# Fourier/Hyena encoder layer: where the first filter taps stand on ScalarE, how six weight halves get their low part, and when stored weight parts leave

## The chip, the cores and the metric

The kernel runs on one core of a Trainium2 chip. The metric is the device time of the program in microseconds (us): the median of three runs. The core's engines work side by side, each through its own list of instructions in a fixed order: TensorE (PE, matmuls), VectorE (DVE), ScalarE (ACT), GpSimd (POOL) and SyncE (SP, which only issues DMAs). DMAs are issued on the queue of SP or of POOL. An engine stops at an instruction whose input isn't there, and all that stands behind that instruction stops with it.

## What is computed

One encoder layer on two sequences of 1024 tokens by 1024 channels, in float32. The reference, cut to the steps that matter here:

```python
xn = rmsnorm(x, g_pre)
p = xn @ w_in
fv, fg, hv, hg, mg = jnp.split(p, [...], axis=-1)
fz = fv.reshape(B, L, F_GROUPS, F_GROUP_DIM)
fz = jnp.fft.fftn(fz, axes=(1, 3), norm="ortho").real        # Fourier branch
y_f = (fz.reshape(B, L, F_WIDTH) * jax.nn.silu(fg)) @ w_fourier_out
hv = short_conv(hv, w_short)                                 # Hyena branch
v, x1, x2 = jnp.split(hv, 3, axis=-1)
h = jnp.sin(f2 * (jnp.sin(f1 * (z @ w1 + b1)) @ w2 + b2))
h = (h @ w3) * jnp.exp(-t * jnp.abs(decay))                  # filter taps
h = h / jnp.sum(jnp.abs(h), axis=(0, 1))
kf = jnp.fft.rfft(two_sided(h))                              # filter spectrum
z = v
for n, gate in enumerate((x1, x2)):
    z = gate * long_conv(z, kf[:, n], hyena_d[n])
y_h = (z * jax.nn.silu(hg)) @ w_hyena_out
g_f, g_h = jnp.split(jax.nn.sigmoid(mg + b_merge), 2, axis=-1)
return x + rmsnorm((g_f * y_f + g_h * y_h) @ w_out, g_post)
```

All of it ends up as matrix products on PE, the Fourier transforms too.

## The kernel before

**Number format.** PE takes float32 rounded to fewer bits ("fp32r"). To keep float32 accuracy each operand is kept as two parts: a high part h, the rounded copy, and a low part l = source - h. A product takes three matmuls, h·h, l·h and h·l. `split` (lines 171 and 181) makes the parts: ACT copies (CAST) and another engine, DVE by default in this region, subtracts.

**Stages.** `phase_fourier` transforms both sequences. For the second, its last stretch goes from about 200 us to 258 us: a product `pfx` (PE, 16 matmuls) fills a small tile that ACT copies to `x5t` (line 411), DVE subtracts a part of it in place, and the closing matmuls of the products `pse` ("alt, x5t") read it. Each product `pse` is copied by ACT to `sev` (line 434), and DVE joins that with the odd half `pso`. The results leave as `d_fz` stores on POOL's queue (lines 486 and 487).

`phase_main` follows, and its opening is interleaved with that last stretch of the Fourier phase:

- `load_x` loads eight tiles of x into xl0_0 to xl0_7 (line 722, SP's queue); ACT casts each into xh0_k (1.04 us), DVE subtracts.
- `hid`, the filter's hidden layer, is loaded, cast by ACT (line 916), and a part of it is subtracted by DVE.
- `filter_taps` runs 16 rounds. A round casts its weights `w3s`, takes the absolute value of `dec` (line 632), does exponentials `ex` (line 643, behind a table load the first time), products `pft` on PE, and multiplications and sums on DVE, and `filter_spectrum` then makes products `pXf`.
- Between the rounds `spill_gate` computes in-projection gates, as filler: one gate in round 0, two in round 1, and so on. In the order in which PE reaches them I call the first five A, B, C, D and E.

**In-projection** (`inproj`, lines 743 to 769). A gate uses two weight half tiles of 128 x 1024 in two pieces, each 128 x 512 values wide. For each: SP loads it raw into `wr` (line 760, two slots, taken in turn), ACT casts it to the high part (line 764), ACT writes its negative into the low part (line 765, "mul"), and POOL issues a DMA that reads the weight from memory once more and adds it to that negative in place (line 766, an accumulating DMA). The high and low part stand in `wh` and `wl` (two slots each) or in one of two single slots for both, `whl`, according to `rooms`, whose turn goes wh, wh, whl (`draw`), whl (`draw2`), and round again. So gate A has wh and wh, gate B the two whl slots, C has wh and wh, D the two whl slots again. PE does 8 matmuls of x with each piece's high and 4 with its low part per 512 columns of tokens: 24 matmuls for a half tile, 48 for a gate.

`keep_parts` (lines 736 to 741): for sections whose parts are needed again for the second sequence, the parts are stored in memory (`d_w`, line 739, POOL's queue), and the stores are issued when the next half tile's accumulating DMA has been issued.

**What sets the order.** The kernel is written as loops; a scheduler with its own model of times then fixes the order of each engine's list. A block `with tc.issue_after(ins)` makes the instructions in it that run on the engine of `ins` stand behind `ins`. The order within SP's and POOL's DMA queues comes from that same step.

Of the kernel before, what the change touches and what calls it, by code (L numbers as in the profile page):

```python
# [9 lines left out]
F32 = mybir.dt.float32  # L10
# [151 lines left out]
class K:  # L162
# [223 lines left out]
    def fourier_half(self, b, half, W, fo, px, pf, begun={}):  # L386

        nc = self.nc
# [5 lines left out]
        for e, (W_, n, X_) in enumerate(((WE, 260, EE), (WO, 256, OO))):  # L394
            for m in range(4):
# [6 lines left out]
                if e == (b + half == 0):  # L402

                    if m == 0:
                        p5 = self.psum("X", 2, "pfx")[0:36, :260]
# [2 lines left out]
                            self.mm(p5, fo["x5"][:, k], WE[i][:, k], k + i == 0, k + i == 8)  # L408

        X5, XX, PX = fo["x5t"], fo["xx"], fo["px"]  # L410
        nc.scalar.copy(X5[0:36], p5)
        self.sub("dve", X5[32:36], p5[32:36], X5[32:36])

        EX = fo["ex"]
# [8 lines left out]
        def stage(np_, data, e, edge, out, tag):  # L423

            pe = self.psum(tag, 2, "pse")[0:np_, :258]
            po = self.psum(tag, 2, "pso")[0:np_, :258]
            for m in range(4):
                last = (edge is None and m == 1) or m == 3
                self.mm3(pe if m < 2 else po, data(m), (seq[:, 0, e, m], seq[:, 1, e, m]), m % 2 == 0, last)
                if m == 1 and edge is not None:  # L430
                    self.mm(pe.rearrange("p (a b) -> p a b", a=3), edge, al, False, True)
            ev = pf.tile([P, 258], F32, tag="sev", name="sev", bufs=1)[0:np_]
            st = pf.tile([P, 514], F32, tag="sst", name="sst", bufs=1)[0:np_]
            nc.scalar.copy(ev, pe)
            self.add("dve", st[:, 0:258], ev, po)
            if e == 0:
                self.sub("dve", st[:, 512:257:-1], ev[:, 0:255], po[:, 0:255])
            else:
                self.stt("dve", st[:, 512:257:-1], ev[:, 0:255], -1.0, po[:, 0:255])
            nc.vector.tensor_copy(st[:, 513:514], st[:, 0:1])  # L440
            if len(out) == 2:
                self.split(out[0], out[1], st, "dve", "act")
            else:
                nc.scalar.copy(out[0][0:34], st)
                self.sub("dve", out[0][32:34], st[32:34], out[0][32:34])
# [3 lines left out]
        for g in range(2):  # L449
            cs = slice(130 * g, 130 * g + P)  # L450
            PP.append(pair([P, 514], "pp", 2))
            stage(P, lambda m: (EE[0][:, m, cs], EE[1][:, m, cs]), 0, X5[:, cs], PP[g], "TX"[g])
        stage(34, lambda m: (EX[0][:, m], EX[1][:, m]), 0, XX, [PX], "T")
        for g in range(2):
            Pp, Qp = PP[g], pair([P, 514], "qp")
            co = slice(P * g, P * g + P)
            stage(P, lambda m: (OO[0][:, m, co], OO[1][:, m, co]), 1, None, Qp, "XT"[g])
            A = pf.tile([P, 1026], F32, tag="fAB", name="fA", bufs=3)
            B = pf.tile([P, 1026], F32, tag="fAB", name="fB", bufs=3)
            gg = 2 * half + g  # L460
            for n in range(2):
# [17 lines left out]
                r = slice(0, w)  # L479
# [3 lines left out]
                r = slice(0, w)  # L483
# [249 lines left out]
        t = pool.tile([P, 2, 512], F32R, tag=tag, name="whl", bufs=1)  # L733
        return [t[:, 0], t[:, 1]]

    def keep_parts(self):

        for t, k in self.unsaved:
            self.nc.gpsimd.dma_start(k, t.bitcast(F32))
        self.unsaved = []  # L740

    def inproj(self, sec, mt, b=None, plain=False):

        nc, a = self.nc, self.a
        ps = [self.psum("mm", 4, f"pin{n}") for n in range(2)]
        for q in range(2):
            s = slice(512 * q, 512 * q + 512)
            src = a["w_in"][sec, mt][:, s]
            kept = self.d_w[sec - 1][mt] if b is not None else None
            if b or plain:  # L750
                h, l = [self.wp.tile([P, 512], F32R, tag=g, name=g, bufs=2) for g in ("wh", "wl")]
            else:
                h, l = self.rooms()
            if b:
                self.keep_parts()
                for t, k in zip((h, l), kept):
                    nc.sync.dma_start(t.bitcast(F32), k[:, s])
            else:
                r = self.wp.tile([P, 512], F32, tag="w", name="wr", bufs=2)
                nc.sync.dma_start(r, src)  # L760
                if plain:
                    self.split(h, l, r, "dve", "act")
                else:
                    nc.scalar.copy(h, r)
                    nc.scalar.mul(l, h, -1.0)
                    self.added = nc.gpsimd.dma_start(l, src, accum_op=ADD)
                    self.keep_parts()
                    if kept:
                        self.unsaved = [(t, k[:, s]) for t, k in zip((h, l), kept)]
            h, l = [t.rearrange("p (a b) -> p a b", a=4) for t in (h, l)]  # L770
            for n in range(2):
                for kk in range(4):
                    k = 4 * q + kk
                    s = slice(512 * n, 512 * n + 512)
                    self.mm3(ps[n], (h[:, kk], l[:, kk]), (self.xh[k][:, s], self.xl[k][:, s]), k == 0, k == 7)
        return ps
# [127 lines left out]
    def phase_main(self, nct=8, nb=NB, nf=16):  # L904
        tc, nc, a = self.tc, self.nc, self.a
        with ExitStack() as es:
            pool = lambda n: es.enter_context(tc.tile_pool(name=n, bufs=1, reuse_waits="tile"))
            mf, wa, wb, mi = pool("mf"), pool("wa"), pool("wb"), pool("mi")
            self.stage2 = pool("m2")
            self.turn, self.unsaved = 3, []  # L910
            ws = Rooms(wa, wb)
            self.load_x(0, range(4))
            self.hid = ws.tile([P, L], F32R, tag="q", name="hid", bufs=2)
            hid = ws.tile([P, L], F32, tag="q", name="hidr", bufs=2)
            nc.sync.dma_start(hid, self.d_h)
            nc.scalar.copy(self.hid, hid)
            self.sub("dve", self.hid[64:128], hid[64:128], self.hid[64:128])
            taps = self.filter_taps(0, 0, ws)
            self.load_x(0, range(4, 8))
            self.cfw0 = mf.tile([P, 4 * P], F32, name="cfw0")  # L920
            self.cfwd = mf.tile([P, 2, 12 * P], F32R, name="cfwd")
            nc.sync.dma_start(self.cfw0, a["c_fw0"])
            nc.gpsimd.tensor_copy(self.cfwd[:, 0, 0:1], self.xl[4][:, 0:1])
            nc.gpsimd.dma_start(self.cfwd, a["c_fwd"])
            for t, n in ((self.th, "c_th"), (self.wsh, "w_short"), (self.bm, "b_merge")):
                nc.sync.dma_start(t, a[n])
            plain = [(5, c) for c in range(8)] + [(6, c) for c in range(8)] + [(4, c) for c in range(NH)]
            fill = sorted([((2 * c + 1) / len(plain), t) for c, t in enumerate(plain)]
                          + [((2 * c + 1) / max(NF, 1), (0, c)) for c in range(NF)])
            fill = [t for _, t in fill]  # L930
            for i in range(nf):
                nxt = self.filter_taps((i + 1) % 2, (i + 1) // 2, ws) if i + 1 < nf else None
                gates = fill[i * len(fill) // nf:(i + 1) * len(fill) // nf]
                if i < nf - 1:
                    self.filter_spectrum(i % 2, i // 2, taps, ws)
                for sec, c in gates:
                    self.spill_gate(0, sec, c, ws)
                if i == nf - 1:
                    first = [self.conv(1 + n, 0, ws, "vx"[n], 0, True) for n in range(2)]
                    self.filter_spectrum(i % 2, i // 2, taps, ws)  # L940
                taps = nxt
                if i == 4:
                    self.cinv = mi.tile([P, 2, INVW], F32R, name="cinv")
                if 4 <= i < 12:
                    w = slice((i - 4) * INVW // 8, (i - 3) * INVW // 8)
                    with tc.issue_after(self.added.ins):
                        nc.gpsimd.dma_start(self.cinv[:, :, w], a["c_inv"][:, :, w])
            self.branches(nb, nct, ws, *first)
# [576 lines left out]
```

## Time and profile before

| quantity | value |
|---|---|
| median of 3 runs | 2421.94 us |
| the runs | 2418.77 to 2423.49 us |
| the profiled execution's own time | 2420.15 us |
| its span in the trace | 2418.3 us |
| busy share of the span: PE, DVE, ACT, POOL | 98 %, 82 %, 47 %, 19 % |

The span is what the trace covers of one execution; 1.85 us lie around it. A row of a timeline has the start in us, the duration in us, the engine, the line of the program, the operation, its output and inputs, shapes, and how many instructions are joined; in brackets stands how long the engine had been idle just before, and what ended that. A row of a window table has the stretch, its length, then the busy us and the count of instructions for PE, PE's weight loads, DVE, ACT and POOL, then the clock that PE was granted (1.00 is full speed), the DMA share and GB/s. A row of the DMA view ends with the size and the median time from issue to landing.

### The profile page before, as it was taken

Reading aid. Unit: us, or ns where it says so; the run is one execution under the profiler, and the core shown is the slowest. Engines: PE = TensorE matmul, PEld = TensorE weight load, DVE = VectorE, ACT = ScalarE, POOL = GpSimd, SP = SyncE. Lnnn points to the kernel's source line nnn. Section 1 sums busy time; section 2 is a strip of 40 time slices with the busy share of each in tenths; the row PEclk is TensorE's granted clock in tenths of the full one; section 3 lists DMA queues with packets and bytes.
Section 4 is the critical chain, followed back from the end, with each engine's and each line's share of the span. In section 5 each row is a group of like instructions: output and inputs, shape, how many; then the busy total and the mean of one; then the engine's idle time right before and its main releaser. Section 6 shows DMA issues by size and latency. Waiting matters only on the chain. (4 is left out here: it accounts for less than half of the span.)

```text
span 2418.3 us, 37119 instructions
## 1 busy us (share of the span) xinstructions
PE 2360.6 (98%) x13006; PEld 2050.7 (85%) x13006; DVE 1976.0 (82%) x3760; ACT 1147.7 (47%) x2140; POOL 447.5 (19%) x575
## 2 busy tenths in 40 slices
PE   6999899999999999999999999999999999999998
PEld 6998788888888888888888888888878888888886
DVE  7786888888737999899899999997666687777787
ACT  6546666666544444344222322333344475656543
POOL 1331111111123332221023454310000000101000
PEclk9999899999999999999999999999999999999999
DMA  7536688787778777666365666553546687888754
GB/s 277 187 127 220 179 222 222 202 225 215 202 219 254 221 223 209 192 177 200 126 194 191 210 218 205 187 179 123 205 158 230 210 298 256 267 270 230 222 159 154
DMA packets 265010, 499.63 MB, mean 207 GB/s; under 512 B 26662, under 2 KB 92423, under 8 KB 264568
## 3 DMA queue, kind: packets, MB, share of 16 engines
q1 hardware_dynamic: 220076, 380.53, 48.0%
q0 software_dynamic: 44560, 116.72, 19.0%
q8 instruction: 102, 1.67, 0.3%
q14 instruction: 84, 0.69, 0.1%
q10 hardware_dynamic: 188, 0.02, 0.0%
HBM read 333.59 MB, written 167.77 MB: 207 GB/s over the span
## 5 line engine op out<-in xcount | busy, mean ns | idle before, releaser
L194 PE MATMUL pin<-xh,wh 128*128 128x512 f32 x1024 | 401.2, 393 | 0.4 <-DMA wh<-d_w 0.4
L194 PE MATMUL pin<-xl,wh 128*128 128x512 f32 x1024 | 401.2, 392 | 0.0
L194 PE MATMUL pin<-xh,wl 128*128 128x512 f32 x1024 | 399.6, 392 | 0.0
L194 PE MATMUL pin<-xh,whl 128*128 128x512 f32 x896 | 292.4, 397 | 8.1 <-DMA whl<-in_w_in 4.5
L194 PEld LDWEIGHTS pin<-xh,wh 128*128 128x128 f32 x1024 | 192.8, 188 | 35.9 <-DMA wh<-d_w 0.8
L194 PEld LDWEIGHTS pin<-xh,wl 128*128 128x128 f32 x1024 | 192.7, 188 | 35.6 <-DMA wl<-in_w_in 0.2
L194 PEld LDWEIGHTS pin<-xl,wh 128*128 128x128 f32 x1024 | 192.7, 188 | 34.8
L194 PEld LDWEIGHTS pin<-xh,whl 128*128 128x128 f32 x896 | 168.3, 190 | 42.8 <-DMA whl<-in_w_in 5.2
L194 PE MATMUL pT<-cinv,yh 128*128 128x256 f32 x1024 | 192.9, 283 | 2.7 <-ACT yh L171 2.7
L194 PE MATMUL pin<-xl,whl 128*128 128x512 f32 x448 | 178.1, 398 | 0.0
L194 PEld LDWEIGHTS pT<-cinv,yh 128*128 128x128 f32 x1024 | 165.4, 191 | 12.9 <-ACT yh L171 3.2
L194 PE MATMUL pX<-bh,cfwd 128*128 128x256 f32 x768 | 159.3, 287 | 0.9 <-ACT bh L171 0.9
L181 DVE TENSOR_TENSOR t<-pX,k 128x1024 f32<-128x1024 f32 x128 | 155.7, 1216 | 3.9 <-PE pX L194 2.9
L171 ACT CAST yh<-y 128x512 fp32r<-128x512 f32 x128 | 79.3, 620 | 152.8 <-DVE y L181 113.1
L194 PE MATMUL pT<-cinv,yl 128*128 128x256 f32 x512 | 145.5, 284 | 0.0
L171 ACT CAST bh<-b 128x512 fp32r<-128x512 f32 x144 | 88.9, 619 | 98.3 <-DVE b L181 58.1
L194 PEld LDWEIGHTS pX<-bh,cfwd 128*128 128x128 f32 x768 | 125.8, 191 | 4.6 <-ACT bh L171 1.3
L181 POOL TENSOR_TENSOR draw<-draw 128x256 f32<-128x256 f32 x96 | 93.8, 977 | 112.1 <-DMA draw<-in_w_out 39.5
L181 DVE TENSOR_TENSOR bl<-b,bh 128x512 fp32r<-128x512 f32 x144 | 100.3, 703 | 11.5 <-ACT bh L171 11.4
L194 PE MATMUL pX<-bl,cfwd 128*128 128x256 f32 x384 | 109.5, 285 | 0.0
L181 DVE TENSOR_TENSOR yl<-y,yh 128x512 fp32r<-128x512 f32 x128 | 90.2, 705 | 16.9 <-ACT yh L171 16.5
L194 PEld LDWEIGHTS pT<-cinv,yl 128*128 128x128 f32 x512 | 98.2, 192 | 1.9
(368 smaller groups left out, 6030.0 us busy)
## 6 DMA issues: line engine op xcount, KB each, us to landing
k<-d_k SPq DMA_DIRECT2D x128, 512.0 KB, 4.6
wr<-in_w_in SPq DMA_DIRECT2D x136, 256.0 KB, 3.6
d_g<-gt SPq DMA_DIRECT2D x92, 256.0 KB, 3.3
d_k<-kt SPq DMA_DIRECT2D x128, 128.0 KB, 3.7
d_k<-kt SPq DMA_DIRECT2D x64, 256.0 KB, 3.6
fz<-d_g SPq DMA_DIRECT2D x64, 256.0 KB, 5.1
wl<-in_w_in POOLq DMA_DIRECT2D x56, 256.0 KB, 5.4
whl<-in_w_in POOLq DMA_DIRECT2D x56, 256.0 KB, 5.7
```

The lines of the kernel that those rows point to most:

```text
L171: self.rounded = nc.scalar.copy(h, src)
L181: return e.tensor_tensor(out, a, b, op=op)
L194: return self.nc.tensor.matmul(out, lhsT, rhs, start=start, stop=stop, skip_group_check=shared)
```

## The change

Three parts. In the first, the cast of `hid` is put behind the copy `x5t` on ACT (`self.edge`), and ACT's part of the first round of `filter_taps` behind the second copy `sev` (`self.evens[1]`). In the second, for the gates of rounds 0 and 1 (A, B and C, six half tiles), `split` is used: the low part is a subtraction by GpSimd from the raw tile and its high part, in place of ACT's negative and the accumulating DMA. In the third, `keep_parts` leaves the newest half tile's stores unissued, so that in the code they come one half tile later than they did.

```diff
@@ -408,7 +408,8 @@
-        nc.scalar.copy(X5[0:36], p5)
+        self.edge = nc.scalar.copy(X5[0:36], p5)
+        self.evens = []
@@ -431,7 +432,7 @@
-            nc.scalar.copy(ev, pe)
+            self.evens.append(nc.scalar.copy(ev, pe))
@@ -733,11 +734,11 @@
-    def keep_parts(self):
+    def keep_parts(self, left=0):
 
-        for t, k in self.unsaved:
-            self.nc.gpsimd.dma_start(k, t.bitcast(F32))
-        self.unsaved = []
+        while len(self.unsaved) > left:
+            for t, k in self.unsaved.pop(0):
+                self.nc.gpsimd.dma_start(k, t.bitcast(F32))
@@ -758,15 +759,14 @@
-                if plain:
-                    self.split(h, l, r, "dve", "act")
+                if plain or self.opening:
+                    self.split(h, l, r, "dve" if plain else "pool", "act")
                 else:
                     nc.scalar.copy(h, r)
                     nc.scalar.mul(l, h, -1.0)
                     self.added = nc.gpsimd.dma_start(l, src, accum_op=ADD)
-                    self.keep_parts()
-                    if kept:
-                        self.unsaved = [(t, k[:, s]) for t, k in zip((h, l), kept)]
+                    self.keep_parts(1)
+                    self.unsaved.append([(t, k[:, s]) for t, k in zip((h, l), kept or ())])
@@ -913,9 +913,11 @@
-            nc.scalar.copy(self.hid, hid)
+            with tc.issue_after(self.edge.ins):
+                nc.scalar.copy(self.hid, hid)
             self.sub("dve", self.hid[64:128], hid[64:128], self.hid[64:128])
-            taps = self.filter_taps(0, 0, ws)
+            with tc.issue_after(self.evens[1].ins):
+                taps = self.filter_taps(0, 0, ws)
@@ -929,6 +931,7 @@
             for i in range(nf):
+                self.opening = i < 2
```

The lines of the changed kernel are one to three higher than those of before from here on.

Three places in the engines' lists show what moves. First, **ACT** where the Fourier copies and the first taps meet (about 204 to 217 us in the trace of before). Before, from the last cast of `oo` on:

```order
L171 CAST oo0_2487<-pfv1_2695 128x256
L916 CAST hid_2985<-hidr_2986 128x1024
L171 CAST w3s_2993<-w3_2990 128x256
L632 ACTIVATE dec_2996<-dec_2996 128x256
L411 CAST x5t_279<-pfx_2516 36x260
L643 ACT_TABLE_LOAD
L643 ACTIVATE ex_3003<-dec_2996,vec_68 128x256 x2
L643 ACTIVATE ex_3013<-dec_2996,vec_68 128x256 x2
L434 COPY sev_2747<-pse_2732 128x258
L171 CAST xh0_0_2965<-xl0_0_2966 128x1024
L434 COPY sev_2772<-pse_2757 128x258
L171 CAST xh0_1_2970<-xl0_1_2971 128x1024
```

And of the change, on the same engine from `x5t` on:

```order
L411 CAST x5t_279<-pfx_2516 36x260
L917 CAST hid_2985<-hidr_2986 128x1024
L435 COPY sev_2747<-pse_2732 128x258
L171 CAST xh0_0_2965<-xl0_0_2966 128x1024
L435 COPY sev_2772<-pse_2757 128x258
L171 CAST w3s_2993<-w3_2990 128x256
L171 CAST pp0_2730<-sst_2748 128x514
L633 ACTIVATE dec_2996<-dec_2996 128x256
L644 ACT_TABLE_LOAD
L644 ACTIVATE ex_3003<-dec_2996,vec_68 128x256 x2
L644 ACTIVATE ex_3013<-dec_2996,vec_68 128x256 x2
L171 CAST xh0_1_2970<-xl0_1_2971 128x1024
```

`x5t` now stands ahead of `hid` and the taps' start; the taps' start stands behind the second `sev`, which itself stands behind the cast of xh0_0; and xh0_1 now stands behind the table load and the exponentials, while xh0_0 keeps its place right behind the first `sev`.

Second, **POOL** (about 190 to 277 us): the accumulating DMAs of the first weight pieces, with the `d_fz` stores between them. Before:

```order
L766 DMA wl_3286<-in_w_in 128x512
L766 DMA wl_3317<-in_w_in 128x512
L766 DMA whl_3554<-in_w_in 128x512
L486 DMA d_fz1_4_105<-fA_2261 128x1024
L487 DMA d_fz1_5_106<-fB_2262 128x1024
...
L766 DMA wl_3631<-in_w_in 128x512
L766 DMA wl_3662<-in_w_in 128x512
L766 DMA whl_3899<-in_w_in 128x512
...
L766 DMA whl_3584<-in_w_in 128x512
L766 DMA wl_3968<-in_w_in 128x512
L766 DMA wl_3999<-in_w_in 128x512
L766 DMA whl_3929<-in_w_in 128x512
```

And of the change (whl_3552 and whl_3581 are B's two pieces, whl_3893 and whl_3923 are D's, wl_3962 and wl_3993 are E's):

```order
L181 TENSOR_TENSOR wl_3286<-wr_3287,wh_3285 128x512
L181 TENSOR_TENSOR wl_3316<-wr_3317,wh_3315 128x512
L181 TENSOR_TENSOR whl_3552<-wr_3553,whl_3552 128x512
L487 DMA d_fz1_4_105<-fA_2261 128x1024
...
L181 TENSOR_TENSOR wl_3627<-wr_3628,wh_3626 128x512
L181 TENSOR_TENSOR wl_3657<-wr_3658,wh_3656 128x512
...
L767 DMA whl_3893<-in_w_in 128x512
...
L181 TENSOR_TENSOR whl_3581<-wr_3582,whl_3581 128x512
L767 DMA wl_3962<-in_w_in 128x512
L767 DMA wl_3993<-in_w_in 128x512
L767 DMA whl_3923<-in_w_in 128x512
```

Six DMAs became six subtractions, in the same places but for D's first piece, which went behind two of the `d_fz` stores. From E's wl on, POOL's list is the same row for row as before, the numbers in the names apart; the stores of line 739 stand where they stood.

Third, **PE** behind gate B's second piece (about 274 to 282 us). Before:

```order
L194 MATMUL pin1_3553<-xh0_7_3071,whl_3584 128x512
L655 MATMUL pn_3143<-acc_3095,ones_73 128x128
L656 MATMUL pn_3143<-ones_73,acc_3095 128x2
L194 MATMUL pft_3365<-w3s_3356,hid_2985 128x256 x4
L194 MATMUL pXf_3195<-b0_3163,cfw0_3076 128x128 x4
L194 MATMUL pXf_3217<-bh_3173,cfwd_3077 128x256
L194 MATMUL pin0_3897<-xh0_0_2965,whl_3899 128x512
```

And of the change, whose first row is the last but one of D's first piece, which there follows on B's second piece directly:

```order
L194 MATMUL pin0_3891<-xl0_3_2981,whl_3893 128x512
L194 MATMUL pin0_3891<-xh0_3_2980,whl_3893 128x512
L194 MATMUL pin0_3891<-xh0_4_3056,whl_3923 128x512
L194 MATMUL pin0_3891<-xl0_4_3057,whl_3923 128x512
L194 MATMUL pXf_3195<-b0_3163,cfw0_3076 128x128 x4
L194 MATMUL pXf_3217<-bh_3173,cfwd_3077 128x256
L194 MATMUL pin0_3891<-xh0_4_3056,whl_3923 128x512
```

The sum `pn`, the products `pft_3365` (now `pft_3363`), the rest of `pXf_3217` and the eight `pft` of two further tiles stood ahead of the matmuls with the low part of D's second piece before, and stand behind them now.

## The prediction

> **What bounds the kernel now.** I read first the page's busy times, then a table of windows, then PE's timeline in the one window that isn't full, then the lists of the engines that PE waits for there.
>
> ```profile
> span 2418.3 us, 37119 instructions
> ...
> PE 2360.6 (98%) x13006; PEld 2050.7 (85%) x13006; DVE 1976.0 (82%) x3760; ACT 1147.7 (47%) x2140; POOL 447.5 (19%) x575
> ```
>
> ```profile
> 200.00:285.00 85.00, 70.52 (x376) 59.65 (x376) 61.67 (x130) 50.03 (x98) 10.05 (x15) 0.88 0.64 197
> 285.00:660.00 375.00, 375.00 (x2077) 326.27 (x2076) 312.48 (x760) 253.60 (x552) 46.84 (x57) 1.00 0.79 216
> ```
>
> PE bounds nearly everything: from 285 to 660 us it is busy for all of 375 us at full clock. The change touches the stretch from 200 to 285 us, where PE stands still for 85 - 70.52 = 14.5 us and has a mean clock of 0.88. By the clock at most 0.12 x 85 = 10 us more are lost, some of it during the idle time. About 20 us are the **ceiling** of what the change can win. Two groups of gaps make it up. The first:
>
> ```profile
> 206.14 0.96 PE L194 MATMUL pse<-seq,ee 128*128 128x258 f32 x6
> 209.56 0.51 PE L194 MATMUL pse<-alt,x5t 128*128 128x258 f32 x2 [2.46 <-DVE x5t L181]
> ...
> 212.38 1.50 PE L194 MATMUL pse<-seq,ex 128*34 128x258 f32 x6 [1.50 <-ACT sev L434]
> ...
> 215.18 1.05 PE L194 MATMUL pin<-xh,wh 128*128 128x512 f32 x2
> ...
> 219.69 0.63 PE L194 MATMUL pin<-xh,wh 128*128 128x512 f32 x2
> ```
>
> PE waits 2.46 us for x5t and 1.50 us for the first sev; at 215.18 gate A starts on tile 0 of x, at 219.69 on tile 1. The second group:
>
> ```profile
> 256.96 0.73 PE L194 MATMUL pft<-w3s,hid 128*128 128x256 f32 x4 [1.40 <-DVE T L181]
> 261.31 0.80 PE L194 MATMUL pin<-xh,whl 128*128 128x512 f32 x1 [3.62 <-ACT whl L764]
> ...
> 267.90 1.22 PE L194 MATMUL pin<-xh,whl 128*128 128x512 f32 x2 [4.51 <-DMA whl<-in_w_in]
> ...
> 274.49 0.38 PE L655 MATMUL pn<-acc,ones 128*128 128x128 f32 x2
> ...
> 275.41 1.05 PE L194 MATMUL pXf<-b,cfw 128*128 128x128 f32 x8
> ...
> 276.42 0.39 PE L194 MATMUL pin<-xh,whl 128*128 128x512 f32 x1
> ...
> 279.68 0.28 PE L194 MATMUL pXf<-bl,cfwd 128*128 128x256 f32 x1
> ...
> 281.96 0.63 PE L194 MATMUL pin<-xh,whl 128*128 128x512 f32 x2
> ```
>
> PE waits 3.62 us for the cast of gate B's second piece (whl) and 4.51 us for the accumulating DMA of its low part. The last row is the low part of gate D's second piece, which waits for nothing.
>
> **First part: the Fourier copies first.** ACT's list there:
>
> ```profile
> 205.75 1.05 ACT L916 CAST hid<-hidr 128x1024 fp32r<-128x1024 f32 x1 [1.72 <-DMA hidr<-d_h]
> 206.71 0.40 ACT L171 CAST w3s<-w 128x256 fp32r<-128x256 f32 x1
> 208.38 0.42 ACT L632 ACTIVATE dec<-dec 128x256 f32<-128x256 f32 x1 [1.27 <-DMA dec<-in_filt_decay]
> 208.70 0.35 ACT L411 CAST x5t<-pfx 36x260 fp32r<-36x260 f32 x1
> 209.07 1.28 ACT L643 ACT_TABLE_LOAD   x1
> 210.37 1.70 ACT L643 ACTIVATE ex<-dec,vec 128x256 f32<-128x256 f32 x4
> ...
> 212.23 1.04 ACT L171 CAST xh<-xl 128x1024 fp32r<-128x1024 f32 x1
> ```
>
> x5t's copy stood behind a wait for `dec`. Now it runs when its product is done, at about 206.2 instead of 208.7, and DVE's subtraction behind it is ready 0.86 us later (209.56 - 208.70), at 207.1, which is when PE is through with the product before it (206.14 + 0.96): the 2.46 us go. Then hid takes 1.05 us on ACT, sev follows at about 207.6, and the product at 212.38 starts near 208.3, **some 4 us earlier**. But what is late next is tile 0:
>
> ```profile
> 204.12 0.43 SPq L722 DMA_DIRECT2D xl<-d_x  x1
> ```
>
> ```profile
> xl<-d_x SPq DMA_DIRECT2D x1, 512.0 KB, 7.8
> ```
>
> It lands at 204.12 + 7.8 = 211.9, as before; its cast ends near 213.0, so gate A starts at 213.0 instead of 215.18. The product itself takes no longer than 215.18 - 212.38 = 2.8, so PE idles from 211.1 or before. Behind that cast, ACT now does sev, w3s (0.40), pp0, dec (0.42), the table load (1.28) and four exponentials (1.70) before it comes to tile 1: 213.0 + 4.3 + 1.05 = 218.4, while PE's work on tile 0, 4.5 us before and some of it at half clock, ends about 217. So gate A starts on tile 1 at 218.4 instead of 219.69: **the first part gains about 1.3 us of the 4**, the rest is waited away for the tiles. Bounds: 4 where PE finds other work, -1 where the cast of tile 1 comes still later.
>
> **POOL's first subtractions.** The row for such an operation, and the stores behind it:
>
> ```profile
> L181 POOL TENSOR_TENSOR x<-x,sg x16: 1291/1718/4405, 766.1 to 1145.2; 128x512 f32<-128x512 f32 x16
> ```
>
> ```profile
> 201.99 0.43 DVE L181 TENSOR_TENSOR fB<-pQ,fPm 128x258 f32<-128x258 f32 x1 [2.68 <-DMA d_fz<-fA]
> ```
>
> ```profile
> d_fz<-fA POOLq DMA_DIRECT2D x1, 512.0 KB, 7.1
> ```
>
> I take 2.0 us for one subtraction, between the bounds 1.3 and 4.4. It reads wr too, so the slot is held 2 us longer and the third load, its subtraction and the d_fz stores queued behind it on POOL come about 2 us later. DVE waits for such a store at 201.99. The store took 7.1 us with three accumulating DMAs ahead of it, which are gone, so it should land as early as before. I take 0; bounds -2.1 (it takes 7.1 again) and +1.0.
>
> **Second part: gate B and what follows it.** The rows of the chain:
>
> ```profile
> 260.65 0.60 ACT L764 CAST whl<-wr 128x512 fp32r<-128x512 f32 x1
> ...
> 262.72 0.61 ACT L765 ACTIVATE whl<-whl 128x512 fp32r<-128x512 f32 x1
> ...
> 268.74 0.62 ACT L764 CAST wh<-wr 128x512 fp32r<-128x512 f32 x1 [2.65 <-DMA wr<-in_w_in]
> ...
> 275.34 0.63 ACT L765 ACTIVATE whl<-whl 128x512 fp32r<-128x512 f32 x1
> ```
>
> ```profile
> 276.26 0.87 POOL L766 DMA_DIRECT2D whl<-in_w_in  x1 [5.09 <-ACT whl L765]
> ```
>
> ```profile
> wr<-in_w_in SPq DMA_DIRECT2D x1, 256.0 KB, 2.9
> ```
>
> ```profile
> wr<-in_w_in SPq DMA_DIRECT2D x1, 256.0 KB, 3.3
> ```
>
> ```profile
> whl<-in_w_in POOLq DMA_DIRECT2D x1, 256.0 KB, 4.7
> ```
>
> The cast moves with the 1.3 us to 259.35 and ends at 259.95; the subtraction ends at 261.95, and PE starts on the low part 5.95 us earlier than at 267.90. It then runs 20 matmuls of B, 12 of D's first piece (which now follows directly), 2 of D's second and the pXf. From 276.42 to 279.68 stand 14 matmuls, 0.233 us each; half that speed until about 4 us after the gap (267.90 was back at full clock near 271.9). So PE ends B near 267.5, D's first piece at 270.4, and the pXf at 272.2. There it meets **a new wait**: the low part of D's second piece is still made by an accumulating DMA. Its price: the load of E's first piece waits for the slot of B's second, freed by the subtraction at 261.95 and no more by the cast at 261.25; it lands at 264.85 (2.9); cast 0.60; E's second load lands at 268.75 (3.3); two casts and two negations stand on ACT, 0.66 each from start to start, until 271.4; POOL issues at 271.6; 4.7 later it is 276.3. PE waits 4.1 us. The same content was reached before at 281.96 less the work that now comes later: 274.49 to 276.42 and 279.68 to 281.96 are 4.2 us, less 1.0 for the pXf that still stands ahead, 3.2. That is 278.8. So the gain there is 278.8 - 276.3 = **2.5 us**, the first part's 1.3 in it. After such a gap the clock has been low:
>
> ```profile
> 268.40:271.80 3.40, 3.40 (x9) 2.63 (x8) 3.27 (x13) 1.25 (x2) 0.85 (x1) 0.50 0.78 161
> ```
>
> 4 us at half clock lose 2.0 us; whether a wait of 4.1 us between busy stretches costs that isn't shown, so 0 to 2.0. The Trainium skill, "TensorE: Matmul & The Clock Gate", Part 1: The HAM clock gate, says that the clock halves after an idle window of about 3.4 us, and that the windows run free of the program: by that rule a wait of 4.1 us costs it only where a whole window falls into it, and the net gain would be 2.5 in most executions. The 0.50 in the row after the 4.51 us wait agrees with it.
>
> **Third part and what is saved.** The stores of parts stand in the same rows of POOL's list, so I count nothing for them (the bounds are the clock's and the chain's). Six negations of 0.6 us leave ACT, which is 47 % busy: nothing.
>
> **Sum.** 2.5 less about half of 0 to 2.0: some **2 us** in the end, since behind 285 us PE is full before and should be after. Profiled execution 2420.15 (span 2418.3 and 1.85 around it) to about 2418.1; from the median of 2421.94 to **2419.9**.
>
> **The rivals.** What a measurement of this kernel can tell from no change is about 0.2 %, 4.84 us.
>
> - *Both gaps close.* D's low part is ready when PE comes (its loads are early since SP has fewer waits), tile 1 isn't waited for. For it: 5.95 us go at 267.90. Against it: the chain of loads above. Without the wait at D, PE is there at 272.2 instead of 278.8: 6.6 us. With the 2.7 of the first part that I have waited away for the tiles, and some clock that isn't lost, 11 us: 2411 to 2415.3. Chance 0.27.
> - *The chain behind GpSimd comes too late (slower).* Place: D's second low part. Price: with a subtraction of 4.4 instead of 2.0 us, loads of 3.6 instead of 2.9 and 3.3, and an accumulating DMA at 5.7 (the page's typical one), it lands at 276.3 + 2.4 + 1.0 + 1.0 = 280.7, and PE loses 280.7 - 278.8 = 1.9 and 2.0 at half clock; with POOL's stores 2.1 us later as well 6.0: 2427.9. It decides from a landing past 278.8. Chance 0.10.
>
> ```profile
> wr<-in_w_in SPq DMA_DIRECT2D x136, 256.0 KB, 3.6
> ...
> whl<-in_w_in POOLq DMA_DIRECT2D x56, 256.0 KB, 5.7
> ```
>
> - *GpSimd against VectorE.* DVE was busy 3.27 of the 3.4 us from 268.40. If a subtraction takes 4.4 us there, and all else goes as I take it, D's part lands at 278.7, the gain is 0.1 less up to 2.0 of clock: 2421.8 to 2423.8. Chance 0.12. The Trainium skill, "GPSIMD Engine Reference", section 1 Specifications, says that GpSimd shares its SBUF interfaces with VectorE and collides with its instructions of two inputs, which speaks against the change; the spread from 1291 to 4405 ns in the row agrees, without showing the cause.
> - *It does less than it says.* The third part does nothing by POOL's list; if the first two only shift waits too, 2420 to 2423. Within the forecast's own spread.
>
> **How the numbers follow.** The forecast with its neighbours (2416 to 2423) has 0.51, of which 0.03 lie under 2417.1, the two late cases have 0.22, both gaps closed 0.27. The range leaves out a tenth on each side: **2412.5 to 2425**. Faster by over 0.2 % 0.30, within 0.60, slower 0.10.
>
> **What would show it.** In the trace of the changed kernel: x5t's copy near 206.2 and no wait of PE for it; a wait of PE for the cast of tile 0 and of tile 1 (213.0, 218.4); the subtraction of B's second piece taking 2 us and PE on its low part near 262; a wait of PE near 272 for the DMA of D's second low part, until 276; and the content of 285 us reached about 2 us earlier. I am wrong if PE doesn't wait for the tiles, if the new wait at D is missing or over 6 us long, or if PE loses time behind 285 us.

## The result: 9 us slower

| | median | runs |
|---|---|---|
| before | 2421.97 us | 2418.77 to 2423.49 (6 runs) |
| changed | 2431.15 us | 2427.25 to 2436.99 (6 runs) |
| ratio | 1.0044 | 95 % interval 1.0034 to 1.0054 |

The same lists of instructions were timed twice more (e2 and e9 below), each time at 1.0027; the mean of the three is 1.0033, some 8 us. The forecast was 2 us faster.

The changed kernel's page and its table of windows:

```profile
span 2429.6 us, 37130 instructions
...
PE 2369.2 (98%) x13006; PEld 2055.8 (85%) x13006; DVE 1982.8 (82%) x3760; ACT 1141.2 (47%) x2134; POOL 451.5 (19%) x575
```

```profile
200.00:285.00 85.00, 72.93 (x373) 61.56 (x372) 57.22 (x120) 45.37 (x90) 12.25 (x15) 0.88 0.57 190
285.00:660.00 375.00, 371.47 (x2060) 321.91 (x2059) 312.02 (x753) 251.88 (x553) 45.52 (x56) 1.00 0.78 213
```

PE stands still for 12.1 us in the opening instead of 14.5, and yet its mean clock there has not risen: by the traces' clock records it has half clock for 20.5 us in both (before from 210.56 to 217.39 and from 258.35 to 272.00 us, changed from 212.47 to 219.30, 260.26 to 267.09 and 277.33 to 284.15). And from 285 to 660 us, where it had been busy throughout, it is idle for 3.5 us. PE's timeline in the opening (at 192 us, where the change hasn't touched a list yet, this execution is 1.5 us later than that of before):

```profile
209.83 0.91 PE L194 MATMUL pso<-seq,ex 128*34 128x258 f32 x6 [0.48 <-DVE sst L441]
214.26 1.22 PE L194 MATMUL pin<-xh,wh 128*128 128x512 f32 x2 [3.53 <-ACT xh L171]
...
220.86 0.63 PE L194 MATMUL pin<-xh,wh 128*128 128x512 f32 x2
...
260.90 0.80 PE L194 MATMUL pin<-xh,whl 128*128 128x512 f32 x1 [2.51 <-ACT whl L171]
...
278.17 1.22 PE L194 MATMUL pin<-xh,whl 128*128 128x512 f32 x2 [3.75 <-DMA whl<-in_w_in]
```

The waits for fB (0.99 us before, at 203.26), x5t and sev are gone; in their place PE waits 3.53 us for tile 0 of x. The wait for B's low part is gone; in its place stands one for D's. Two windows of this trace, behind the first and behind the second of these waits:

```profile
214.20:219.10 4.90, 4.83 (x14) 4.11 (x15) 2.99 (x6) 4.87 (x11) 0.00 (x0) 0.50 1.03 421
```

```profile
278.00:282.00 4.00, 3.83 (x9) 3.06 (x10) 0.00 (x0) 0.59 (x1) 0.00 (x0) 0.50 0.18 68
```

Half clock behind each. In the filter rounds PE has five idle rows over 0.3 us, where the trace of before has none:

```profile
437.00 0.46 PE L656 MATMUL pn<-acc,ones 128*128 128x128 f32 x2 [1.14 <-DVE acc L181]
452.99 1.13 PE L194 MATMUL pXf<-b,cfw 128*128 128x128 f32 x8 [0.83 <-DVE b L181]
454.62 0.39 PE L194 MATMUL pXf<-bh,cfwd 128*128 128x256 f32 x1 [0.50 <-ACT bh L171]
482.11 0.39 PE L194 MATMUL pXf<-bh,cfwd 128*128 128x256 f32 x1 [0.42 <-ACT bh L171]
493.51 0.35 PE L194 MATMUL pXf<-bh,cfwd 128*128 128x256 f32 x1 [0.55 <-ACT gt L804]
```

Followed back, the first comes from DVE, and DVE's from ACT:

```profile
433.71 0.69 DVE L181 TENSOR_TENSOR acc<-acc,ex 128x512 f32<-128x512 f32 x1 [2.63 <-ACT ex L647]
```

```profile
431.80 0.42 ACT L633 ACTIVATE dec<-dec 128x256 f32<-128x256 f32 x1 [3.33 <-DMA dec<-in_filt_decay]
432.25 0.91 ACT L644 ACTIVATE ex<-dec,vec 128x256 f32<-128x256 f32 x2
```

ACT waits 3.33 us for the decay, with exponentials and an absolute value that DVE needs queued behind. The decay has a single slot, so its load is issued when the last exponentials of the round before have read it. ACT waited at this place before too, for 1.75 us (in the trace of before at 426.15); but there the round's last absolute value stood ahead of the decay, at 423.77, and in this arrangement it stands behind the decay and two exponentials, at 433.06.

Which instructions stand where is the scheduler's work. The change moves rows on all engines up to about 640 us: of the 13006 matmuls in PE's trace, by their names, the first 1320 and those from the 3702nd on (635 us in the trace of before) stand where they stood, of ACT's 2142 rows the first 216 and those from the 843rd on. Behind that the lists of both kernels are the same on all engines.

### The profile page after: what moved, and what is told of

The parts are those of the page before. It is cut to its first block, busy times and chain, and to the rows that moved or that the text cites. A ratio compares the mean times of both kernels' runs of the same rounds, so it can differ in the third digit from the quotient of the medians.

```text
span 2429.6 us, 37130 instructions
## 1 busy us (share of the span) xinstructions
PE 2369.2 (98%) x13006; PEld 2055.8 (85%) x13006; DVE 1982.8 (82%) x3760; ACT 1141.2 (47%) x2134; POOL 451.5 (19%) x575
## 5 line engine op out<-in xcount | busy, mean ns | idle before, releaser
L194 PEld LDWEIGHTS pin<-xl,whl 128*128 128x128 f32 x448 | 85.9, 192 | 16.9
```

What stands on the lines that cost most here:

```text
L194: return self.nc.tensor.matmul(out, lhsT, rhs, start=start, stop=stop, skip_group_check=shared)
```

## The experiments

To compare traces by stage I take points at which PE has done the same matmuls, by name, in every trace: at 192, 331, 648 and 1661 us of the first trace of before. At 192 us the lists haven't parted yet, and from 648 us on they are the same again. The table's three columns say by how many us each stretch between these points took longer than in that trace. They stand for one execution each, the ratio for all timed ones; the traces of e5, e9, e10 and e11 are of the fastest execution of their series. For the noise: up to the first point the traces lie up to 1.4 us ahead of the first trace of before and up to 2.7 behind it.

| trace | opening, 192 to 331 us | rounds, to 648 us | behind, to 1661 us | ratio, interval |
|---|---|---|---|---|
| before, 2nd (e1) and 3rd (e15) | -0.1, -1.4 | 0.0, 0.0 | -2.0, -1.7 | 0.9996 (0.9986 to 1.0005) |
| changed, 1st | +0.8 | +5.3 | +3.5 | 1.0044 |
| changed, e2 | -0.3 | +4.7 | +3.9 | 1.0027 (1.0017 to 1.0037) |
| changed, e9 | -2.4 | +5.1 | +1.9 | 1.0027 (1.0017 to 1.0038) |
| changed, e14 | -1.0 | +5.2 | +9.3 | one run |
| e3, first part alone | -2.4 | -0.2 | +1.8 | 1.0000 (0.9990 to 1.0011) |
| e4, second part alone | -3.7 | +1.6 | +0.6 | 1.0009 (0.9999 to 1.0018) |
| e5 | -1.9 | +3.2 | -3.3 | 1.0013 (1.0004 to 1.0022) |
| e6, rounds 0 to 2 subtracted | -5.0 | +2.1 | +0.9 | 0.9998 (0.9988 to 1.0007) |
| e7 | -2.1 | +3.5 | +2.4 | 1.0011 (1.0002 to 1.0020) |
| e8 | +0.5 | +3.3 | +1.9 | 1.0011 (1.0003 to 1.0020) |
| e10 | +0.2 | +0.6 | -2.6 | 1.0012 (1.0002 to 1.0023) |
| e11 | -2.4 | +0.1 | +0.7 | 1.0010 (1.0000 to 1.0020) |
| e12, one dec | -1.2 | -0.1 | -0.9 | 0.9999 (0.9990 to 1.0009) |
| e13, all rounds subtracted | -5.4 | +7.1 | -3.0 | 1.0012 (0.9996 to 1.0027) |

PE's idle rows show only a part of what the rounds lose (3.4 of 5.3 us in the first trace of the changed kernel), because the profile models where a matmul ends: from the start of the last matmul ahead of the first of the five rows, at 435.47, to that row's start at 437.00 are 1.53 us, where 0.23 are usual, and the row shows 1.14 as idle.

**e1: the third part alone.** Its edit is that of `keep_parts` and `unsaved`; no row moves on any engine.

> The third part alone (stores of weight parts kept one half tile longer in the code). The lists of all five engines are row for row those of before. Theory: it does nothing, ratio 1.000 within its interval, and this run's trace shows how far two executions of the same lists differ. Rival: the third part costs something in the branches, between 1000 and 1520 us, where the changed kernel falls back by another 4 us: then it would be here too, ratio 1.002.

0.9996 (0.9986 to 1.0005): it does nothing. The scheduler puts a store where its data is ready, and one half tile later in the code changes no place.

**e2: the first two parts without the third.** The lists are the changed kernel's.

> The first and second part without the third: the lists are row for row those of the changed kernel. Theory: the whole loss is here, ratio 1.0044 (about 9 us), and a second trace of the same lists shows which of its losses come again: about 2 us by 285 us and 4 to 5 us between 430 and 510 us should, the 4 us between 960 and 1520 us only if they come from the lists and not from chance. Rival: without the third part the loss is halved, 1.002.

1.0027. The loss in the rounds comes again (+4.7), and so does, against what I held possible as chance, the one behind them (+3.9).

**e3: the first part alone.**

```diff
-            nc.scalar.copy(self.hid, hid)
+            with tc.issue_after(self.edge.ins):
+                nc.scalar.copy(self.hid, hid)
-            taps = self.filter_taps(0, 0, ws)
+            with tc.issue_after(self.evens[1].ins):
+                taps = self.filter_taps(0, 0, ws)
```

> The first part alone (x5t ahead of the first taps). Theory that the lists of the filter rounds make most of the loss: this too rearranges them from 216 rows of ACT on, so it gains some 2 us by 224 us and then loses or wins by its own arrangement, anything between -4 and +6 us, with PE's idle rows between 300 and 660 us telling which. Rival that GpSimd's subtractions make the loss: faster than before by 1 to 3 us (0.999), no idle rows behind 285 us.

The opening gains 2.4 us, the rounds lose nothing, and the time isn't changed (1.0000): the 1.8 us behind took most of it back in this trace. What it shows is how the opening behaves without subtractions; PE's timeline and three windows:

```profile
205.02 0.62 PE L194 MATMUL pQ<-qp,chan 128*128 128x256 f32 x3 [2.11 <-DVE fB L177]
...
213.36 0.63 PE L194 MATMUL pin<-xh,wh 128*128 128x512 f32 x2
...
218.20 0.73 PE L194 MATMUL pin<-xh,wh 128*128 128x512 f32 x2 [0.43 <-ACT xh L171]
```

```profile
202.83:206.24 3.41, 1.30 (x11) 1.19 (x11) 1.63 (x5) 0.73 (x2) 0.00 (x0) 1.00 0.66 224
206.24:209.65 3.41, 3.41 (x19) 2.94 (x17) 1.54 (x6) 0.44 (x2) 1.05 (x2) 0.50 0.67 241
...
212.00:216.00 4.00, 3.53 (x23) 2.97 (x22) 3.61 (x9) 3.92 (x8) 0.00 (x0) 1.00 1.02 396
```

Here PE still waits 2.11 us at 205.02 (for fB, for which DVE waits until a d_fz store has landed). Half clock follows that wait for 3.41 us, but ahead of tile 0, for which PE would have had to wait anyway. PE comes to tile 0 just when that is cast, at full clock again, and reaches tile 1 at 218.20. The changed kernel comes to fB some 2 us earlier and waits for no store there; it stands still for 3.53 us in one piece at 214.26 instead, works at half clock for 5.0 us behind that (to 219.30), and reaches tile 1 at 220.86. At 221 us, with the same matmuls done, e3 is 2.9 us ahead of before and the changed kernel 1.2: **the earlier stores bring 2 us that the tile takes back, and half clock behind the tile takes 1.7 us more.**

**e4: the second part alone** (the edit is that of `inproj`, with `opening`).

> The second part alone (six low parts by GpSimd's subtraction). Theory: the wait for gate B's low part (4.5 us) goes, a wait at gate D's low part of about 4 us comes, near 0 by 285 us; then PE's idle rows between 300 and 660 us by its own arrangement of the lists. Rival that GpSimd's subtractions make the loss: slower by 6 to 10 us (1.003 to 1.004), VectorE's instructions beside a subtraction longer than in before.

Its opening gains 3.7 us, its rounds have no idle row over 0.3 us but lose 1.6, and the ratio is 1.0009. PE's wait for D's low part is 1.30 us here, and no half clock follows:

```profile
277.33 0.73 PE L194 MATMUL pin<-xh,whl 128*128 128x512 f32 x2 [1.30 <-DMA whl<-in_w_in]
```

So the parts alone came out at 0 and some 2 us slower (the interval of e4 reaches 1.0018, 4.4 us), and the two together lose some 8.

**e5 and e8: hid behind x5t, the taps not held**, e5 with the subtractions of rounds 0 and 1, e8 also of round 2.

```diff
+            with tc.issue_after(self.edge.ins):
+                nc.scalar.copy(self.hid, hid)
             taps = self.filter_taps(0, 0, ws)
```

> The second part, and of the first only the hid cast behind x5t; the first taps on ACT are not held behind the second sev copy. The opening has the same six subtractions, but the scheduler arranges the filter rounds anew. Theory that the arrangement of the rounds makes half of the loss: PE's idle rows between 300 and 700 us (3.4 and 2.3 us in two traces of the changed lists, 0 in before and in each part alone) go or differ, and the ratio lies between 0.999 and 1.002. Rival that the loss comes from the opening's subtractions and x5t together, whatever the lists: idle rows near 437 and 453 us again and 1.003.

> Subtraction in rounds 0 to 2, hid behind x5t, taps not held: a third arrangement of the same opening. Theory: opening 4 to 7 us ahead of before at 300 us (x5t's 2.5 us and D's wait gone), rounds by their arrangement, ratio 0.997 to 1.000. Rival: as for the two before.

e5: 1.0013, PE's idle rows in the rounds 1.1 us instead of 2.3 to 3.5. Its lists behind the opening are those of e4, which had no such row and lost 1.6 us in the rounds, not 3.2: so the same rows can wait in one execution and not in another. e8: 1.0011, against a forecast of 0.997 to 1.000; its opening didn't gain the 4 to 7 us: without the hold on the taps, `dec` and ACT's wait of 2.47 us for its load stay ahead of x5t, and PE waits 3.85 us for it.

**e6 and e7: the subtraction in round 2 too**, so that D's low part needs no DMA; e6 with the first part, e7 without.

```diff
-                self.opening = i < 2
+                self.opening = i < 3
```

> The changed kernel (without its third part, which moves nothing) with GpSimd's subtraction in round 2 too, so that gate D's low part and E's are subtracted and not accumulated by DMA. Theory: PE's wait of 3.6 us for D's low part and the 5 us at half clock behind it go, 4 to 6 us by 300 us against the changed kernel; then the rounds by their own arrangement, ratio to before 0.997 to 1.001. Rival that a subtraction on GpSimd itself costs: more of them, slower than the changed kernel, 1.004 or over.

> As the one before, but x5t and the first taps where they stood: the subtractions of rounds 0 to 2 alone. Theory: against the second part alone (1.0009; 2 to 3.5 us ahead of before at 300 us) its wait of 1.3 us for D goes, so 3 to 6 us ahead at 300 us, ratio 0.997 to 1.000 unless the rounds fall badly. Rival: as above, slower than the second part alone.

In e6 the wait for D is gone and the clock is full:

```profile
276.00:280.00 4.00, 4.00 (x33) 3.83 (x33) 4.00 (x12) 2.06 (x5) 0.00 (x0) 1.00 0.17 66
```

Its opening is 5.0 us ahead of before where the changed kernel's four traces have a mean of -0.7, and the ratio is 0.9998. More subtractions cost nothing here; D's accumulating DMA did. e7 came out at 1.0011, against a forecast of 0.997 to 1.000, with 3.5 us lost in its own arrangement of the rounds.

**e9 and e14: the changed kernel again**, **e15: before again**, for more traces of the same lists.

> The changed kernel again, for a third trace of its lists and a second time. Theory: about 1 us behind before by 300 us, another 3 to 4 us lost between 410 and 510 us (2 to 3.5 us of idle rows of PE, the first at pn near 435 us behind ACT's wait for dec), ratio 1.003 to 1.0045. What it also tells: the two traces of these lists lost 4.7 us between 700 and 1540 us, where the lists are those of before; if that comes again it belongs to the change, if it is within -2 to +4 us as in the other kernels' traces, it is chance.

> The changed kernel once more, for a fourth trace. Theory: 2 to 3.5 us of idle rows between 430 and 500 us again. Between 700 and 1620 us: 2.3 to 5 us lost again if that belongs to the change, anything from -2 to +4 if it is chance.

> The kernel before once more, for a third trace of its lists: no idle rows between 300 and 700 us; between 700 and 1620 us it stands within 2 us of the first trace.

The five idle rows of PE between 430 and 495 us come at the same places in e9 and e14, and three of them in e2: 3.4, 2.3, 2.7 and 3.5 us together over the four traces, none in the three of before. The rounds as a whole lose 4.7 to 5.3 us in the four traces, and in the three of before they agree within 0.1 us. Behind 648 us the changed kernel loses 3.5, 3.9, 1.9 and 9.3 us, the three traces of before spread over 2.0, the ten others over -3.3 to +2.4. Three of the four lie outside all others, so that loss probably belongs to the changed kernel too, though its lists there are those of before; it isn't shown, since e9's 1.9 us lie below the 2.3 that I had set as the mark. In the opening e9 has another face:

```profile
276.23 0.72 PE L194 MATMUL pin<-xh,whl 128*128 128x512 f32 x2 [1.41 <-DMA whl<-in_w_in]
```

```profile
276.00:280.00 4.00, 3.77 (x22) 3.36 (x23) 1.44 (x6) 1.14 (x3) 0.00 (x0) 1.00 0.21 75
```

The same part lands within half a us of the same time, PE came 2 us later and waited 1.41 us, and the clock stayed full behind it. PE was later because it had waited 1.78 us for DVE at 268.74 and then had half clock, from 269.61 to 273.03: ahead of the DMA's landing that costs nothing.

**e10 and e11: the same opening, other rounds.** The gates of round 5, or of round 3, are subtracted on GpSimd too. By their names, PE's matmuls come in the changed kernel's order up to 354 us (e10) and 310 us (e11) of its trace.

```diff
-                self.opening = i < 2
+                self.opening = i < 2 or i == 5
```

> The changed kernel with the gates of round 5 subtracted on GpSimd too. PE's list is the changed kernel's up to its row 1967 (about 328 us), so the opening is the same; behind it the scheduler arranges the rounds anew up to row 3480. Theory that the arrangement of the rounds makes the loss at 410 to 510 us: the first 328 us as in the changed kernel (1 us behind before), then idle rows of another size at other places, 0 to 2 us lost there instead of 3 to 4, ratio 1.0005 to 1.003. Rival that the opening carries its delay forward: idle rows near 435 and 452 us again, 1.0035.

> The same with round 3 instead of round 5: PE's list is the changed kernel's up to row 1731 (about 280 us). Theory and rival as for the one before: the opening's wait for D's low part is there in both, the idle rows at 430 to 500 us are not those of the changed kernel.

```profile
410.00:510.00 100.00, 100.00 (x562) 87.29 (x561) 88.82 (x216) 73.19 (x161) 13.73 (x18) 1.00 0.84 226
```

In this window of e10 PE is busy throughout, where the changed kernel has 96.47 us of 100; e11 has no idle row between 300 and 700 us. Their rounds lose 0.6 and 0.1 us, with openings inside the changed kernel's range (+0.2 and -2.4 in -2.4 to +0.8). Ratios 1.0012 and 1.0010, against 1.0027 for the changed kernel in the same series of runs (e9). **The loss in the rounds lies in how the rows of the rounds are arranged**, and isn't carried over from the opening. (Each edit also swaps some gates' negations and DMAs for subtractions; e13, which swaps nearly all, shows that this by itself doesn't help the rounds.)

**e12: one decay for all rounds.**

```diff
+        if n == ct == 0:
+            self.dec = ws.tile([P, 256], F32, tag="dec", name="dec", bufs=1)
+            nc.sync.dma_start(self.dec, a["filt_decay"][n, ct].partition_broadcast(P))
+            nc.scalar.activation(self.dec, self.dec, AF.Abs)
+        dec = self.dec
```

> The changed kernel with the decay loaded and made absolute once, in the first round, and used by all rounds: leaves out 15 loads of dec and 15 absolute values of ACT. Theory that the idle rows of PE at pn come from dec's single slot (its load can't be issued before the last exponential of the round before, which stands late in ACT's list): ACT's waits of 1.1 to 3.5 us for dec are gone and PE's idle rows between 300 and 700 us are under 0.5 us; ratio 1.000 to 1.0015 with the opening's loss left. Rival that DVE's waits for the d_k stores make them: idle rows stay at 2 us or more.

It leaves out 15 loads and some 6 us of ACT's work, so all rounds use the first round's decay and it doesn't compute the layer. No idle row of PE between 300 and 700 us, and 0.9999: the decay's load and slot are in the chain that makes them. But it also rearranges the rounds, so it doesn't show that they alone do it; e10 and e11 kept them, with waits of ACT for dec of 0.5 to 4.1 us, and had nearly no idle row.

**e13: all rounds but the last subtracted.**

> The changed kernel with GpSimd's subtraction in rounds 0 to 14, so that no accumulating DMA is left in the filter rounds, and no negation on ACT. Theory: gate D's wait is gone as in the run with rounds 0 to 2 (5 us ahead of before at 290 us), and as each low part needs no second load, PE's idle rows between 300 and 700 us stay under 1.2 us by arrangement: ratio 0.997 to 1.0005. Rival that subtractions beside VectorE's work cost: VectorE's idle and PE's idle rows grow in every round, ratio 1.003 or over.

1.0012 (0.9996 to 1.0027), against a forecast of 0.997 to 1.0005: no gain to be measured. The opening is the best of all (-5.4), and the rounds are the worst (+7.1), with idle rows of PE for the same sum `pn` as in the changed kernel and 3.41 us at half clock behind each:

```profile
408.06 0.46 PE L656 MATMUL pn<-acc,ones 128*128 128x128 f32 x2 [1.94 <-DVE acc L181]
435.02 0.46 PE L656 MATMUL pn<-acc,ones 128*128 128x128 f32 x2 [1.87 <-DVE acc L181]
```

No version beat before by more than its measurement is uncertain; e6, 0.9998, stands level with it.

## Why the prediction was wrong

- **x5t's copy at about 206.2, no wait for it: right**, and earlier still (206.42 - 1.5 = 204.9), since the wait for fB went too. The product behind the first sev came 5.5 us earlier (208.36 - 1.5 = 206.9, forecast 208.3), and tile 0 took it back.
- **The first part's 1.3 us: near in size, by another way.** I let PE end its work on tile 0 near 217 and wait for tile 1 until 218.4. In none of the four traces does it wait for tile 1, which I had named as a sign of being wrong. It worked at half clock for 5 us behind the wait for tile 0 and did six matmuls of `pso` first, which before stood behind the start of tile 1, and reached tile 1 at 220.86 - 1.5 = 219.4. With the same matmuls done, at 221 us, the changed kernel is 0.8 to 1.2 us ahead of the first trace of before; the other two traces of before are 0.3 and 1.1 ahead of it as well, so little of this is clear of chance.
- **POOL's stores, counted at nothing: they came earlier**, and DVE's wait of 2.68 us for them went down to 1.02. That lengthened PE's idle stretch ahead of tile 0 and was no gain.
- **A subtraction of 2.0 us: too dear**, in the useful direction; the four into wl took 1.30 us each, and B's second piece, beside VectorE's work, 1.74 (the profile's groups on POOL, and its timeline):

```profile
L181 POOL TENSOR_TENSOR wl<-wr,wh 128x512 fp32r<-128x512 f32 x4 | 5.1, 1298 | 23.1 <-ACT wh L171 15.1 <-PE pQ L194 8.0
```

```profile
260.93 1.74 POOL L181 TENSOR_TENSOR whl<-wr,whl 128x512 fp32r<-128x512 f32 x1 [4.20 <-ACT whl L171]
```

- **The new wait at D: right in place and time.** Forecast: PE there at 272.2, part landed at 276.3, 4.1 us of wait. Measured, less 1.5: the landing at 276.7, after a wait of 3.75 (3.58, 1.41 and 3.09 in e2, e9 and e14). The issue was earlier than I had it (271.87 - 1.5 = 270.4 against 271.6), the landing longer, 6.3 us instead of 4.7 (5.4 to 6.3 in the four traces); here three such DMAs left within 5 us, before within 10:

```profile
271.87 0.85 POOL L767 DMA_DIRECT2D whl<-in_w_in  x1 [0.28 <-issue]
```

```profile
whl<-in_w_in POOLq DMA_DIRECT2D x1, 256.0 KB, 6.3
```

- **The clock behind it, 0 to 2.0 us: too narrow.** In the first trace PE works at half clock for 5.98 us behind the wait (to 284.15), which loses 3.0 us; in e2 and e14 for 3.1 and 3.0 us, in e9 not at all. My row at 268.40 was no sign for it either way: half clock had begun at 258.35 in that trace, ahead of the wait of 4.51 us. With the same matmuls done at 331 us the opening stands at -0.7 us on the mean of four traces (-2.4 to +0.8) instead of -2, and before itself at 0, -0.1 and -1.4.
- **"Behind 285 us PE is full before and should be after": the step that failed**, a loss put at nothing without a reason. The rounds lost 5.1 us on the mean of four traces (4.7 to 5.3). The change rearranges the rounds up to 640 us, and I took a PE that is busy throughout as a sign of slack. It is only the sign that this one arrangement had enough; ACT waits for dec and DVE for ACT in the rounds, and a new arrangement draws anew: the rounds of e3, e11 and e12 lose nothing, those of e10 0.6, of e4 to e8 1.6 to 3.5, of the changed kernel 4.7 to 5.3, of e13 7.1.
- **The third part, nothing: right** (e1).
- **The slower rival** had the wrong place: it wanted D's part to land past 278.8, and it landed in time. What makes the kernel slower lies behind the opening.

**What stays open.** Behind 648 us the changed lists lose 1.9 to 9.3 us in four traces, nearly as much as the rounds on the mean, with the same lists as before. The traces show where: but for 0.7 us it falls between 936 and 1008 us and between 1271 and 1532 us, where PE waits in other kernels too. From 936 to 1008 us e14 loses 5.7 us, with three times 3.41 us at half clock, where the three traces of before have it never or once. Two of the larger idle rows, of the changed kernel and of e14, wait for a stored weight part:

```profile
1285.64 0.50 PE L194 MATMUL pin<-xh,wl 128*128 128x512 f32 x1 [1.24 <-DMA wl<-d_w]
```

```profile
1286.37 0.50 PE L194 MATMUL pin<-xh,wl 128*128 128x512 f32 x1 [1.58 <-DMA wl<-d_w]
```

But e5 (1.18) and e12 (1.56) wait there too without such a loss, and e9 doesn't wait. How far the engines stand apart at 648 us, or what the DMAs carry then, may be the cause; no run here separates it. Nor was a second slot for the decay tried.

## What to carry to other kernels

Where a scheduler orders the lists, an edit in one place is an edit of everything that it rearranges behind it: compare the lists to their end, and count every rearranged stage as a risk of some us, above all one in which the bounding engine is just full, since a full engine doesn't show how little slack its suppliers have. A wait that is removed in front of a fixed arrival (here a 512 KB tile at 212 us) moves on to that arrival, and half clock can take more of the gain: 1.7 us less was left here than in e3. And when a serial chain is shortened at one link (B's low part), do the next link of the same kind too (D's): round 2 was worth some 4 us of the opening.

## What the runs showed of the hardware

- **What idle time costs in clock.** In the clock records of all 17 traces half clock comes in pieces of 3.41 us, whose boundaries lie on one raster of 3.41 us through a whole trace. How long PE was idle in the piece before decides. From 20 us on full clock was lost 106 times, each time behind a piece with 1.73 us of idle PE or more; 2.0 us always lost it, 1.73 to 1.96 us sometimes, less never. Out of half clock PE came only behind a piece with 0.62 us of idle time or less. So waits of 1.30 us in e4 and 1.41 in e9 cost no clock, but 1.78 in e9 and 2.11 in e3 did, far shorter than the 3.53 and 3.75 of the first trace. e9's pieces, and two of the first trace of the changed kernel around the wait at 260.90:

```profile
266.20:269.61 3.41, 1.63 (x8) 1.03 (x7) 3.41 (x9) 2.64 (x5) 0.89 (x1) 1.00 0.86 215
269.61:273.03 3.42, 3.42 (x10) 2.67 (x9) 3.42 (x15) 1.90 (x4) 1.72 (x2) 0.50 0.91 217
273.03:276.44 3.41, 2.00 (x14) 1.68 (x13) 2.86 (x7) 1.48 (x4) 0.00 (x0) 1.00 0.78 176
276.44:279.85 3.41, 3.41 (x21) 3.00 (x21) 0.85 (x5) 0.62 (x2) 0.00 (x0) 1.00 0.23 82
```

```profile
256.85:260.26 3.41, 1.30 (x9) 0.89 (x8) 2.86 (x7) 3.41 (x9) 0.00 (x0) 1.00 0.79 306
260.26:263.67 3.41, 2.77 (x6) 2.00 (x7) 3.41 (x5) 0.59 (x2) 1.74 (x1) 0.50 0.42 88
```

  The Trainium skill, "TensorE: Matmul & The Clock Gate", Part 1: The HAM clock gate, has the clock halve after an idle window of about 3.4 us with windows that run free, and remarks that the count of slow matmuls varies from run to run. The length of the pieces, their raster and that variation agree with it; that the whole window has to be idle doesn't, since about half of it was enough here.
- **GpSimd beside VectorE.** With 56 subtractions in the rounds (e13), one of the 28 into `whl` took 1.27 us at the least, 1.46 as the median and 6.06 at the most:

```profile
L181 POOL TENSOR_TENSOR whl<-wr,whl x28: 1272/1460/6057, 195.5 to 636.4; 128x512 fp32r<-128x512 f32 x28
```

The Trainium skill, "GPSIMD Engine Reference", section 1 Specifications, says that GpSimd shares its SBUF interfaces with VectorE. The spread agrees; that a collision makes it wasn't measured by itself.
